# An encoder trunk's down-projection: the sums of its weights are transferred at half the rate

## The chip, the cores and the metric

The kernel runs on one core of a Trainium2 chip. The metric is the device time of one execution in microseconds. The time before is the median of three runs. A profile is one further execution, taken with the hardware profiler; its times count from the start of its span.

## The reference

Two layers of an encoder, on 512 tokens with 1024 channels, in float32. Each layer normalises x, makes one wide projection, runs four branches on it (a convolution and three kinds of attention), weighs each branch with gates from the same projection, adds them, projects once more and adds the result to x. A feed-forward part follows:

```python
def _conv_ffn(h, w_up, conv_w, conv_b, w_down):
    u = _depthwise_conv(h @ w_up, conv_w, conv_b)
    gate, up = jnp.split(u, 2, axis=-1)
    return (jax.nn.silu(gate) * up) @ w_down

# in each layer:
    branch = jnp.einsum('bsnc,ncd->bsnd', ys, w_branch[l])
    gates = jax.nn.sigmoid(gate_pre.reshape(bsz, seq, N_BRANCH, D_MODEL) + gate_b[l])
    mixed = jnp.sum(gates * branch, axis=2)
    x = x + mixed @ w_out[l]
    x = x + _conv_ffn(_rmsnorm(x, g_ffn[l]), w_up[l], ffn_conv_w[l], ffn_conv_b[l], w_down[l])
```

`w_down` is 2816 x 1024. The change concerns sums of blocks of this matrix, which the kernel makes because it multiplies blocks in a scheme with seven products instead of eight.

## The kernel before

**Products.** A float32 operand is split into a high part that TensorE takes exactly and a low part that holds the rest, and each product is three matmuls: high x high, high x low, low x high (`prod`, L273 to L275). A *block* is one unit of weights (128 x 1024) against all eight tiles of the activations: 24 matmuls of 512 columns. Weights come through the SP queue (L248) into two buffers, ScalarE makes the high part (L252), VectorE the low part (L254).

**The down-projection's sums.** `w_down` is held in eleven slabs of 128 rows by 2048 columns, each made of four blocks of 512 columns, b11, b12, b21 and b22. The scheme of seven products needs four sums of them in each slab: s3 = b12 + b11, s1 = b11 + b21, s2 = s3 + b21 and s4 = s2 + b22. They don't depend on the data, but they are made on the chip, from DRAM to DRAM: a plain transfer writes the first term, an accumulating transfer adds the next. `weight_sums` issues them for three chunks, of 4, 4 and 3 slabs, so that a transfer moves 512, 512 or 384 rows of 512 numbers: 1, 1 and 0.75 MB. A layer has 24 of them: in this order three for s3 = b12, three for s1 = b11, three that add b11 to s3, three that add b21 to s1, three copies s2 = s3, three that add b21, three copies s4 = s2, three that add b22. All go through GpSimd's queue (L1133), and since they belong to one queue, whatever GpSimd has to wait for before it issues one holds up all that stands behind it there. `quarter_sums` (L1110) does the like for the up-projection, 40 transfers a layer, and comes first.

**What sets the order.** The kernel is written as one main sequence of TensorE's work with generators at its side. After each half block the main sequence calls `tick`, and `tick` lets each generator in the list `side` take one step; what the step records stands at that place in the program. `slowly` wraps both generators of sums. It lets twelve ticks go by, and then as many ticks after each transfer as the generator yields (one, where it yields nothing):

```python
    def slowly(self, g):
        for _ in range(12):
            yield
        for n in g:
            for _ in range(n or SLOW):
                yield
```

`paced` makes each transfer wait, on the chip, for the matmul that was recorded last before it. In `layer` the sums are put into `side` at the start of the attention stage. Then come the remaining projections, and three stages of gates, `gates(n)` for three of the four branches. After them stands `while self.side: self.tick()`: it calls `tick` again and again, with no work of TensorE between, until every generator in the list has ended. The fourth `gates` follows, then the output projection and the feed-forward part.

**What stands behind the sums on GpSimd.** `gates` makes, for each of eight tiles d, a block for the gate, and VectorE scales it (L849, `t`). Two blocks later `branch` multiplies the branch's output by its weights, VectorE joins gate and product (L878, again a `t`; there are two buffers of that kind), and the result is added to the running sum `mx` (L879). In the second and third stage, and in the fourth for d below 6, GpSimd does this addition. In the fourth stage ScalarE and VectorE then split the sum into `mh` and `ml` (L883, L884) for the output projection. TensorE's results stand in four PSUM banks of the kind `mm` until VectorE has read them.

Of the kernel before, what the change touches and what calls it, by code (L numbers as in the profile page):

```python
# [218 lines left out]
class Trunk:  # L219
# [911 lines left out]
    def weight_sums(self, l):  # L1131

        add = lambda *a, **k: self.paced(self.nc.gpsimd.dma_start(*a, **k))  # L1133
        items = []
        for c in range(0, NP2, CHUNK):
            n = min(CHUNK, NP2 - c)
            t = self.dram.tile([n * P, 4 * S], F32, name=f"sums{c}", tag=f"sums{c}", bufs=2)
            self.sums[l].append(t)
            src = self.all_quads[l][c * P:(c + n) * P]
            part = lambda x, i: x[:, i * S:(i + 1) * S]  # L1140
            items.append((part, t, src))
        s2, s1, s3, s4 = range(4)
        b11, b12, b21, b22 = range(4)
        for d, s in ((s3, b12), (s1, b11)):
            for part, t, src in items:
                add(part(t, d), part(src, s))
                yield 2
        for d, s in ((s3, b11), (s1, b21)):
            for part, t, src in items:
                add(part(t, d), part(src, s), accum_op=ALU.add)  # L1150
                yield 2
        for d, b, s in ((s2, s3, b21), (s4, s2, b22)):
            for part, t, src in items:
                add(part(t, d), part(t, b))
                yield 2
            for part, t, src in items:
                add(part(t, d), part(src, s), accum_op=ALU.add)
                yield 2

    def pair_tags(self, j):  # L1160

# [366 lines left out]
```

## Time and profile before

| | us |
|---|---|
| median of 3 runs | 1598.54 (1597.10 to 1599.13) |
| the profiled execution | 1600.03 |
| its span | 1598.3 |
| TensorE busy | 1547.3 (97%) |
| VectorE busy | 1252.9 (78%) |
| ScalarE busy | 895.3 (56%) |
| GpSimd busy | 204.3 (13%) |
| software queue of the DMA engines (GpSimd's) | 92.81 MB, 26.0% of 16 engines |
| hardware queue (SP's) | 212.10 MB, 41.6% |

In the profile PE is TensorE's matmul, PEld its weight load, DVE is VectorE, ACT ScalarE, POOL GpSimd and SP SyncE. A row of a timeline gives start and duration in us, the engine, the line and the tile that is written, and in brackets how long the engine sat idle before and what released it. The duration of a DMA row on POOL is the time to issue it, not to transfer it. A row of the DMA view gives the size of a transfer and the time from issue to landing. q0 is the queue of the transfers that GpSimd issues, q1 that of SyncE's.

### The profile page before, as it was taken

To read this page: it belongs to the slowest core of one execution; us is meant where nothing else is said; L and a number is where in the kernel's file an instruction comes from. 1 tells how busy PE (TensorE), PEld (TensorE's weight loads), DVE (VectorE), ACT (ScalarE), POOL (GpSimd) and SP (SyncE) were. 2 spreads that over 40 slices of the span, in tenths; PEclk is the share of its full clock that TensorE was granted. 3 is DMA by queue.
4 is the path that set the end of the run, shared out by engine and by line. 5 is a ranking of instruction groups with operands and counts; after the bars stand their busy time and mean duration, and the time that the engine had idled before them with its cause. 6 is when DMAs were issued, how large, how long until landed. Compare 5 with 4: busy or idle time off the path is not lost.

```text
span 1598.3 us, 21942 instructions
## 1 busy us (share of the span) xinstructions
PE 1547.3 (97%) x7842; PEld 1312.7 (82%) x7842; DVE 1252.9 (78%) x2114; ACT 895.3 (56%) x1504; POOL 204.3 (13%) x308
## 2 busy tenths in 40 slices
PE   9999999996999999999999999999969999899999
PEld 8888888884889988888888878888858898888887
DVE  6699988752689989895676989887446888899964
ACT  6778777332456655563557677763234555554642
POOL 0044112332100000000002231132221000000000
PEclk9999999998999999999999999999989999999999
DMA  7789786999654543366567978769986466633565
GB/s 234 225 226 244 190 204 191 214 230 231 202 177 132 175 160 128 93 202 203 178 195 224 242 208 198 197 186 234 245 204 222 158 166 187 185 122 104 174 215 172
DMA packets 124797, 306.84 MB, mean 192 GB/s; under 512 B 28176, under 2 KB 30096, under 8 KB 124688
## 3 DMA queue, kind: packets, MB, share of 16 engines
q1 hardware_dynamic: 93712, 212.10, 41.6%
q0 software_dynamic: 30688, 92.81, 26.0%
q8 instruction: 62, 1.02, 0.3%
q10 hardware_dynamic: 288, 0.52, 0.1%
q14 instruction: 47, 0.39, 0.1%
HBM read 287.56 MB, written 100.67 MB: 243 GB/s over the span
## 4 chain that ended last, share of the span: by engine, by line
PE 73%; DMA 10%; DVE 9%; ACT 5%; issue 2%; POOL 1%; ACTq 0%; DVEq 0%; POOLq 0%
PE mm L273 14%; PE mm L275 14%; PE mm L274 14%; PE aux L992 4%; DVE w_lo L254 3%; DMA w_raw<-W 3%; DMA w_raw<-qS 3%; DMA sums<-W 3%; PE aux L1224 2%; PE aux L1223 2%; PE aux L1225 2%; ACT w_hi L252 2%; PE mm L1224 2%; PE mm L1223 2%; PE mm L1225 2%
## 5 line engine op out<-in xcount | busy, mean ns | idle before, releaser
L252 ACT ACTIVATE w_hi<-w_raw 128x1024 fp32r<-128x1024 f32 (+1 forms) x335 | 350.6, 1047 | 360.9 <-PE mm L274 127.9
L254 DVE TENSOR_TENSOR w_lo<-w_raw,w_hi 128x1024 fp32r<-128x1024 f32 (+1 forms) x335 | 406.3, 1215 | 110.3 <-ACT w_hi L252 108.6
L273 PE MATMUL mm<-xh,w_hi 128*128 128x512 f32 x960 | 377.0, 393 | 28.1 <-DVE t L849 27.1
L275 PE MATMUL mm<-xh,w_lo 128*128 128x512 f32 x960 | 375.8, 391 | 0.0
L274 PE MATMUL mm<-xl,w_hi 128*128 128x512 f32 x960 | 375.4, 391 | 0.0
L273 PEld LDWEIGHTS mm<-xh,w_hi 128*128 128x128 f32 x960 | 181.2, 189 | 65.9 <-ACT w_hi L252 27.9
L275 PEld LDWEIGHTS mm<-xh,w_lo 128*128 128x128 f32 x960 | 180.8, 188 | 39.5 <-DVE w_lo L254 1.4
L274 PEld LDWEIGHTS mm<-xl,w_hi 128*128 128x128 f32 x960 | 181.3, 189 | 36.2
L992 PE MATMUL aux<-form,w_hi 128*128 128x256 f32 x640 | 117.2, 284 | 1.3 <-ACT w_hi L252 1.1
L992 PEld LDWEIGHTS aux<-form,w_hi 128*128 128x128 f32 x640 | 99.8, 192 | 2.3 <-ACT w_hi L252 2.1
L440 DVE SCALAR_TENSOR_TENSOR cv<-cv,prm 128x512 f32<-128x512 f32 x120 | 94.0, 783 | 0.7
L992 PE MATMUL aux<-form,w_lo 128*128 128x256 f32 x320 | 91.0, 285 | 2.5 <-DVE w_lo L254 2.5
L1033 ACT ACTIVATE cy<-U,prm 128x512 f32<-128x512 f32 x88 | 69.9, 806 | 26.2 <-DVE U L1017 14.3
L879 POOL TENSOR_TENSOR mx<-mx,t 128x512 f32<-128x512 f32 x44 | 63.1, 1440 | 133.6 <-DVE t L878 133.5
L502 PE MATMUL mm<-w_hi,xh 128*128 128x512 f32 x192 | 76.4, 398 | 0.4 <-DVE V L630 0.4
L503 PE MATMUL mm<-w_lo,xh 128*128 128x512 f32 x192 | 75.0, 390 | 0.0
L504 PE MATMUL mm<-w_hi,xl 128*128 128x512 f32 x192 | 74.8, 390 | 0.0
L1110 POOL DMA_DIRECT2D qS<-W x60 | 43.7, 728 | 218.0 <-PE aux L780 107.2
L767 ACT ACTIVATE e<-e,rl 128x256 f32<-128x256 f32 (+2 forms) x96 | 57.4, 598 | 22.0 <-DVE rl L766 21.5
L1034 DVE SCALAR_TENSOR_TENSOR cy<-U,prm,cy 128x512 f32<-128x512 f32 x88 | 64.7, 745 | 6.2 <-ACT cy L1033 6.2
L849 DVE TENSOR_TENSOR t<-mm,RB 128x512 f32<-128x512 f32 x64 | 43.8, 685 | 29.3 <-PE mm L275 29.2
L1035 DVE SCALAR_TENSOR_TENSOR cy<-U,prm,cy 128x512 f32<-128x512 f32 x88 | 64.8, 745 | 0.8
(339 smaller groups left out, 3193.0 us busy)
## 6 DMA issues: line engine op xcount, KB each, us to landing
w_raw<-W SPq DMA_DIRECT2D x213, 512.0 KB, 3.7
qS<-W POOLq DMA_DIRECT2D x60, 512.0 KB, 6.4
sums<-W POOLq DMA_DIRECT2D x24, 1024.0 KB, 13.7
w_raw<-qS SPq DMA_DIRECT2D x40, 512.0 KB, 3.5
w_raw<-W SPq DMA_DIRECT2D x66, 256.0 KB, 3.9
w_raw<-sums SPq DMA_DIRECT2D x44, 256.0 KB, 4.0
w_raw<-sums SPq DMA_DIRECT2D x22, 512.0 KB, 4.6
qS<-qS POOLq DMA_DIRECT2D x20, 512.0 KB, 4.8
```

The lines of the kernel that those rows point to most:

```text
L252: w = nc.scalar.activation(hi[:, s], raw[:, s], AF.Copy)
L254: nc.vector.tensor_tensor(lo[:, s], raw[:, s], hi[:, s].bitcast(F32), ALU.subtract)
L273: mm(ps, lhsT=wh, rhs=xh, start=start, stop=False)
L274: mm(ps, lhsT=wh, rhs=xl, start=False, stop=False)
L275: self.last_mm = mm(ps, lhsT=wl, rhs=xh, start=False, stop=stop)
L440: self.after_mm(v.scalar_tensor_tensor(acc, u[:, t:t + S], w(t), acc, ALU.mult, ALU.add))
L502: mm(pss[b], lhsT=self.Xh[k][:, t], rhs=hi[:, s], start=k == 0, stop=False)
L503: mm(pss[b], lhsT=self.Xh[k][:, t], rhs=lo[:, s], start=False, stop=False)
L504: self.last_mm = mm(pss[b], lhsT=self.Xl[k][:, t], rhs=hi[:, s], start=False, stop=k == KT - 1)
L992: self.last_mm = nc.tensor.matmul(o, lhsT=w[:, s], rhs=x, start=start and not (e or j or i), stop=j == 3 and i == 2, skip_group_check=True)
L1033: nc.scalar.activation(y, u[:, 1:513], AF.Identity, scale=w(1), bias=self.par('ffn_conv_b', c))
L1035: v.scalar_tensor_tensor(y, u[:, 2:514], w(2), y, ALU.mult, ALU.add)
```

## The change

In `weight_sums` each `yield 2` becomes `yield 4`: after each of the 24 transfers the generator lets four ticks go by instead of two.

```diff
         for d, s in ((s3, b12), (s1, b11)):
             for part, t, src in items:
                 add(part(t, d), part(src, s))
-                yield 2
+                yield 4
         for d, s in ((s3, b11), (s1, b21)):
             for part, t, src in items:
                 add(part(t, d), part(src, s), accum_op=ALU.add)
-                yield 2
+                yield 4
         for d, b, s in ((s2, s3, b21), (s4, s2, b22)):
             for part, t, src in items:
                 add(part(t, d), part(t, b))
-                yield 2
+                yield 4
             for part, t, src in items:
                 add(part(t, d), part(src, s), accum_op=ALU.add)
-                yield 2
+                yield 4
```

How this moves the instructions is seen on GpSimd's queue alone; on the other engines the same instructions stand in the same order. First the end of the three gate stages in layer 0, before the change. The three tiles sums_2681 to sums_2683 are the three chunks; `W` as source is a block of the weights, `sums` as source is a copy; PE_49 is the wait for a matmul, DMASW with a number the wait for an earlier transfer of this queue, DVE_49 the wait for VectorE:

```order
L1133 DMA sums_2681<-sums_2681 512x512 [waits DMASW0_49,PE_49]
L879 TENSOR_TENSOR mx<-mx,t_3629 128x512 [waits DVE_49]
L879 TENSOR_TENSOR mx<-mx,t_3707 128x512 [waits DVE_49]
L1133 DMA sums_2682<-sums_2682 512x512 [waits DMASW1_49,PE_49]
L879 TENSOR_TENSOR mx<-mx,t_3753 128x512 [waits DVE_49]
L879 TENSOR_TENSOR mx<-mx,t_3763 128x512 [waits DVE_49,Pool_49]
L1133 DMA sums_2683<-sums_2683 384x512 [waits DMASW2_49,PE_49]
L879 TENSOR_TENSOR mx<-mx,t_3773 128x512 [waits DVE_49]
L1133 DMA sums_2681<-W 512x512 [waits DMASW6_49]
L1133 DMA sums_2682<-W 512x512 [waits DMASW7_49]
L1133 DMA sums_2683<-W 384x512 [waits DMASW3_49,DMASW0_49]
```

The same place with the change:

```order
L1133 DMA sums_2681<-W 512x512 [waits DMASW2_49,DMASW0_49,PE_49]
L879 TENSOR_TENSOR mx<-mx,t_3623 128x512 [waits DVE_49]
L879 TENSOR_TENSOR mx<-mx,t_3701 128x512 [waits DVE_49]
L879 TENSOR_TENSOR mx<-mx,t_3746 128x512 [waits DVE_49]
L879 TENSOR_TENSOR mx<-mx,t_3756 128x512 [waits DVE_49,Pool_49]
L1133 DMA sums_2682<-W 512x512 [waits DMASW3_49,DMASW1_49,PE_49]
L879 TENSOR_TENSOR mx<-mx,t_3766 128x512 [waits DVE_49]
L1133 DMA sums_2683<-W 384x512 [waits DMASW4_49]
L1133 DMA sums_2681<-W 512x512 [waits DMASW5_49]
L1133 DMA sums_2682<-W 512x512 [waits DMASW6_49]
L1133 DMA sums_2683<-W 384x512 [waits DMASW7_49]
```

Where three copies of s2 stood among the additions, the 13th to the 15th transfer, now the 7th and the 8th stand. The rows without PE_49 are those that the loop behind the third stage records: before, they begin with the 16th transfer, now with the 9th.

The second place is where both end, in layer 0, on GpSimd's queue with the change; the first row is the copy that makes s4 for the first chunk, the 19th transfer:

```order
L1133 DMA sums_2681<-sums_2681 512x512 [waits DMASW4_49,DMASW1_49]
L1133 DMA sums_2682<-sums_2682 512x512 [waits DMASW5_49,DMASW2_49]
L1133 DMA sums_2683<-sums_2683 384x512 [waits DMASW3_49]
L1133 DMA sums_2681<-W 512x512 [waits DMASW4_49]
L1133 DMA sums_2682<-W 512x512 [waits DMASW5_49]
L1133 DMA sums_2683<-W 384x512 [waits DMASW6_49]
L879 TENSOR_TENSOR mx<-mx,t_3908 128x512 [waits DVE_49,Pool_49]
L879 TENSOR_TENSOR mx<-mx,t_3957 128x512 [waits DVE_49,Pool_49]
```

These rows are the same before and after: the 19th to the 24th transfer stand in one piece ahead of the first addition of the fourth gate stage, and each waits for a transfer that was issued three places ahead of it. In layer 1 the same rows stand in the same way.

## The prediction

> **What bounds the kernel now.** I read the page's busy times first, then what TensorE (PE) waited for, then a table of stretches, and then GpSimd (POOL) instruction by instruction at the one place where TensorE stands still. First the page, then the three largest rows of TensorE's waits over the whole span (total us, how often, longest):
>
> ```profile
> PE 1547.3 (97%) x7842; PEld 1312.7 (82%) x7842; DVE 1252.9 (78%) x2114; ACT 895.3 (56%) x1504; POOL 204.3 (13%) x308
> ```
>
> ```profile
> PE mm L273 <- DVE t L849: 27.1, 2, 14.9
> PE aux L992 <- DVE w_lo L254: 4.7, 8, 1.3
> PE mm L992 <- ACT w_hi L252: 3.3, 2, 1.8
> ```
>
> TensorE is the bound, and more than half of what it loses is two stalls of 14.9 and 12.2 us. The table of stretches (length, busy us of PE, PEld, DVE, ACT, POOL, granted clock, DMA share, GB/s) places them:
>
> ```profile
> 220.00:230.00 10.00, 10.00 (x52) 8.35 (x51) 8.56 (x20) 8.80 (x27) 2.32 (x3) 1.00 1.01 223
> ...
> 330.00:340.00 10.00, 10.00 (x45) 8.27 (x45) 7.61 (x10) 5.25 (x8) 4.21 (x4) 1.00 0.74 222
> ...
> 370.00:380.00 10.00, 0.00 (x0) 0.00 (x0) 0.00 (x0) 0.00 (x0) 3.99 (x5) 0.62 1.03 236
> ...
> 1160.00:1170.00 10.00, 1.21 (x6) 0.67 (x4) 0.00 (x0) 0.00 (x0) 3.65 (x5) 0.71 0.99 254
> ```
>
> From 220 to 340, where the sums of layer 0 are issued now, all twelve stretches of 10 us have TensorE busy throughout; a lighter load on the DMA engines has nothing to give there. At 370 TensorE, VectorE and ScalarE all stand still and only POOL and the DMA engines work; layer 1 repeats it at 1160. The timeline of POOL over the drain of layer 0 (start, duration, instruction, and in brackets its idle time and what ended it):
>
> ```profile
> 340.16 0.59 POOL L1133 DMA_DIRECT2D sums<-sums  x1
> 340.77 1.68 POOL L879 TENSOR_TENSOR mx<-mx,t 128x512 f32<-128x512 f32 x1
> 342.39 2.12 POOL L1133 DMA_DIRECT2D sums<-W  x2
> 347.02 0.95 POOL L1133 DMA_DIRECT2D sums<-W  x1 [2.51 <-DMA sums<-sums]
> 358.24 0.66 POOL L1133 DMA_DIRECT2D sums<-sums  x1 [10.26 <-DMA sums<-W]
> 365.40 0.65 POOL L1133 DMA_DIRECT2D sums<-sums  x1 [6.51 <-DMA sums<-W]
> 369.72 0.59 POOL L1133 DMA_DIRECT2D sums<-sums  x1 [3.67 <-DMA sums<-W]
> ...
> 378.41 0.95 POOL L1133 DMA_DIRECT2D sums<-W  x1 [1.09 <-DMA sums<-sums]
> 379.02 1.63 POOL L879 TENSOR_TENSOR mx<-mx,t 128x512 f32<-128x512 f32 x1
> ```
>
> Number a layer's 24 sum transfers 1 to 24, in the order of the code: 1-6 plain, 7-12 accumulating, 13-15 copies, 16-18 accumulating, 19-21 copies, 22-24 accumulating; each three are 1, 1 and 0.75 MB. The row at 340.16 is number 15, and 16 to 24 follow with nothing between them: the loop that ends the third gate stage empties the pacing generator at once. Each of them waits on POOL until an earlier transfer has landed, and behind number 24 stands the addition L879 of the last gate stage. From there the timelines of VectorE and TensorE carry it on:
>
> ```profile
> 357.50 0.68 DVE L878 SCALAR_TENSOR_TENSOR t<-th,mm 128x512 f32<-128x512 f32 x1
> 381.34 0.69 DVE L884 SCALAR_TENSOR_TENSOR ml<-mx,mh 128x512 fp32r<-128x512 f32 x1 [23.16 <-ACT mh L883]
> ```
>
> ```profile
> 367.44 0.39 PE L275 MATMUL mm<-yh,w_lo 128*128 128x512 f32 x1
> 382.78 0.77 PE L273 MATMUL mm<-xh,w_hi 128*128 128x512 f32 x1 [14.95 <-DVE t L849]
> ```
>
> VectorE gives its product at 358.2, then stands at L884, which needs ScalarE's L883, which needs POOL's L879. Everything later in VectorE's queue (the evacuations L849, the weight splits L254) stands behind it. TensorE goes on until its four PSUM banks are full, at 367.8, and comes back 3.8 us after POOL reaches L879. So **each us by which POOL comes later to that first L879 is a us of TensorE**, with no slack left.
>
> **The change part by part.** *What it moves.* A step after four half blocks stands where every second step stood: the rows of the order show number 8 in the place of number 15, the one at 340.16, in both layers. So 1 to 8 are paced and 9 to 24 are emptied at once: sixteen transfers, not nine. No transfer is added or taken away; on TensorE, VectorE, ScalarE and the SP queue every instruction stays in its place. The first reads of `sums` stay safe: the SP queue issues them here, 75 us behind L879, and both shift together, while 24 is issued just ahead of L879 and needs some 18 us:
>
> ```profile
> 454.35 0.86 SPq L248 DMA_DIRECT2D w_raw<-sums  x2
> ```
>
> ```profile
> sums<-W POOLq DMA_DIRECT2D x1, 768.0 KB, 17.6
> ```
>
> *What stands between 340.16 and L879.* Number 24 is issued when 21 has landed (it waits for the lane of 21; 378.0 and 378.41 above). Now the queue has to carry 15 to 21 in that time; then it has to carry 8 to 21. Added: 8 to 12, accumulating, 1 + 0.75 + 1 + 1 + 0.75 = 4.5 MB, and the copies 13 and 14, 2 MB.
>
> *What a MB costs.* For each transfer of the drain of layer 0, its row of the DMA view (size, us from issue to landing; number 17 from the chain of waits: start, us), in order 15, 16, 17, 18, 19, 20, 21:
>
> ```profile
> sums<-sums POOLq DMA_DIRECT2D x1, 768.0 KB, 6.5
> ...
> sums<-W POOLq DMA_DIRECT2D x1, 1024.0 KB, 15.4
> ...
> 343.05 21.96 DMA sums<-W
> ...
> sums<-W POOLq DMA_DIRECT2D x1, 768.0 KB, 22.3
> ...
> sums<-sums POOLq DMA_DIRECT2D x1, 1024.0 KB, 14.4
> ...
> sums<-sums POOLq DMA_DIRECT2D x1, 1024.0 KB, 10.5
> ...
> sums<-sums POOLq DMA_DIRECT2D x1, 768.0 KB, 8.3
> ```
>
> With the issue times above they land at 346.7, 357.8, 365.0, 369.3, 372.6, 375.9 and 378.0: one after the other, a queue that is never empty. So the cost of one is the distance between landings. Accumulating: 15 to 17 took 18.3 us for 2 MB, 9.2 us a MB; 16 to 17 alone 7.2; 17 to 18 took 4.3 us for 0.75 MB, 5.7 a MB. Copies: 369.3 to 378.0, 8.7 us for 2.75 MB, 3.2 a MB. Why the first are dear shows in the queues' share of the DMA engines (packets, MB, share), first from 346 to 358, then from 365 to 369:
>
> ```profile
> q0 software_dynamic: 654, 1.31, 77.0%
> q1 hardware_dynamic: 325, 1.17, 26.1%
> ```
>
> ```profile
> q0 software_dynamic: 394, 1.14, 110.7%
> q1 hardware_dynamic: 2, 0.00, 0.3%
> ```
>
> The weight loads (q1) compete until VectorE's stop has filled their buffers; then the sums have the engines alone. That many weight loads are made now and after the change, so the 6.5 MB that come on top fall into the time in which the queue is alone. I take the row of that time, 5.7 us a MB: 4.5 x 5.7 + 2 x 3.2 = 25.7 + 6.4 = **32 us in layer 0**. In layer 1 the same rows of timeline, chain and DMA view (18 issued at 1140.69, 21 at 1161.27):
>
> ```profile
> 1136.17 20.72 DMA sums<-W
> ```
>
> ```profile
> 1140.69 0.94 POOL L1133 DMA_DIRECT2D sums<-W  x1 [3.06 <-DMA sums<-sums]
> ...
> 1161.27 0.59 POOL L1133 DMA_DIRECT2D sums<-sums  x1 [3.32 <-DMA sums<-W]
> ```
>
> ```profile
> sums<-W POOLq DMA_DIRECT2D x1, 768.0 KB, 20.2
> ...
> sums<-sums POOLq DMA_DIRECT2D x1, 768.0 KB, 7.4
> ```
>
> 17 lands at 1156.9, 18 at 1160.9, 21 at 1168.7: 5.3 us a MB accumulating, 2.8 a copy; 4.5 x 5.3 + 2 x 2.8 = 23.9 + 5.6 = **29.5 us in layer 1**. Together 61 us.
>
> *Bounds.* From below, accumulating transfers that run at the copies' pace in the longer queue: 6.5 x 3.2 and 6.5 x 2.8, 39 us. From above, all 4.5 MB at the disturbed price of 9.2: 2 x (41.4 + 6.4), 96 us. I choose near the row of the undisturbed queue, since nothing runs beside it there.
>
> *What I cost at nothing.* The restart. The granted clock is already down to 0.62 in the present stall, and this stretch behind it pays for it today:
>
> ```profile
> 380.00:390.00 10.00, 7.22 (x25) 5.57 (x26) 6.04 (x8) 4.61 (x6) 2.28 (x3) 0.70 1.10 228
> ```
>
> A longer stall pays that once as well; were it not paid already, it would be some 0.3 x 7.2 = 2 us. The lighter DMA load from 220 to 340: TensorE has no idle time there to give back. Numbers 22 to 24 and the weight loads behind them meet as they do now, only later.
>
> The profiled execution took 1600.03 us; 1600.0 + 61 = 1661, and since it stands 1.5 above the median of the runs, **1660** for the median.
>
> **The rivals.** *A. The long queue goes faster.* For it: with five transfers in line instead of three, the read and write of an accumulation could overlap better; then 39 us, 1638. Against: the queue already had all of the engines' time, 110.7%, when it made 5.7 us a MB. The Trainium skill, "DMA: Bandwidth & Descriptors", section "Anatomy of one DMA — SWDGE (gpsimd) path", fits such a transfer by 2.0 us and its bytes over 436 GB/s, with no word on accumulation: an estimate from it is 6.8 million bytes / 436 GB/s = 16 us a layer, 1630 in all. By that figure, 0.75 MB behind another transfer would take 1.8 us; the trace has 4.3 for an accumulation, so it does not agree.
>
> *B. The disturbed price holds throughout.* If weight loads, or the source reads of deeper accumulations, keep the price at 7.2 to 9.2, the sum is 2 x (32.4 + 6.4) = 78 to 96 us, 1676 to 1694. Against: no weight can be loaded while VectorE stands.
>
> *C. The stalls go away (the other side).* Were numbers 9 to 24 to find their predecessors landed, they would cost POOL only their issue: sixteen at 0.6 to 1.0 us, some 14 us, from 342.9 to 357. That is when VectorE's product is ready, so L879 would not be late, both stalls would vanish, and the time would be 1598.5 - 27 = 1571. It decides as soon as 21 lands before 357. For it: 1 to 7 have had more time each to land. Against: 16, 19 and 22 each need the one before in the same chunk, and 19 to 21 cannot start before 16 to 18 have been carried, which alone took until 369.3 with less ahead of them.
>
> *D. The change does not reach the drain.* If the remaining steps were paced on through the last gate stage, POOL would have no block at all. The order excludes it: sixteen rows of sums ahead of L879.
>
> **How the numbers follow.** The forecast, 1648 to 1674: 0.72. A, around 1638: 0.10. B, 1676 to 1694: 0.15. C and D, not slower: 0.03. The range 1643 to 1682 leaves out most of A, the dearer half of B, and C, not quite 2 in 10. A measurement of this kernel tells a difference of about 0.2%, 3 us, from no change; every case but C and D is far beyond it: slower 0.97, within 0.2% 0.01, faster 0.02.
>
> **What would show it.** TensorE's wait for L849 should again be two, near 47 and 42 us, some 88 in all instead of 27.1, and no other wait should have grown. POOL should issue an accumulating transfer where it now issues the copy at 340.16, then its first L879 of the last gate stage near 379 + 32 = 411. In layer 1 number 21 should land near 1168.7 + 61.5 = 1230. Number 21 should land about 70 us behind number 8's issue, not 38. The landings of 9 to 18 with the hardware queue silent show the price: 5.3 to 5.7 us a MB is the forecast, near 3 is A, over 7 is B. I am wrong in kind if TensorE idles elsewhere, or if POOL reaches L879 before 379.

## The result, and the profile after

With one transfer per four half blocks the kernel takes 1663.2 us (median of four runs, 1660.2 to 1664.9) against 1598.8 for the kernel before on the same chip: 1.0402 times as long, with an interval of 1.0383 to 1.0421. The profiled execution took 1664.91 us, its span 1663.1.

The page of the changed kernel and TensorE's largest waits:

```profile
PE 1549.0 (93%) x7842; PEld 1313.8 (79%) x7842; DVE 1252.5 (75%) x2114; ACT 895.2 (54%) x1504; POOL 204.9 (12%) x308
```

```profile
PE mm L273 <- DVE t L849: 88.5, 2, 44.4
PE aux L992 <- DVE w_lo L254: 5.3, 7, 1.3
PE aux L992 <- ACT w_hi L252: 4.3, 6, 1.0
```

TensorE's work is what it was, 1549 us. The wait for L849 has gone from 27.1 to 88.5 us, and it is still two stalls: 44.4 us in layer 0, and so 44.1 in layer 1. These 61.4 us are 95% of the 64.8 by which the span has grown; of the other 3.4, 1.7 are busy time and the rest small waits.

The same stretch of GpSimd as before, from the last paced transfer (number 8) to the first addition of the fourth gate stage:

```profile
336.83 1.02 POOL L1133 DMA_DIRECT2D sums<-W  x1
337.51 1.66 POOL L879 TENSOR_TENSOR mx<-mx,t 128x512 f32<-128x512 f32 x1
339.06 3.10 POOL L1133 DMA_DIRECT2D sums<-W  x3
352.11 0.95 POOL L1133 DMA_DIRECT2D sums<-W  x1 [9.94 <-issue]
356.02 1.32 POOL L1133 DMA_DIRECT2D sums<-sums  x2 [2.97 <-issue]
364.44 0.59 POOL L1133 DMA_DIRECT2D sums<-sums  x1 [7.10 <-issue]
376.94 1.05 POOL L1133 DMA_DIRECT2D sums<-W  x1 [11.90 <-DMA sums<-sums]
...
381.27 0.95 POOL L1133 DMA_DIRECT2D sums<-W  x1 [0.82 <-DMA sums<-sums]
389.51 0.66 POOL L1133 DMA_DIRECT2D sums<-sums  x1 [7.29 <-DMA sums<-W]
...
398.43 0.59 POOL L1133 DMA_DIRECT2D sums<-sums  x1 [3.17 <-DMA sums<-W]
...
406.96 0.95 POOL L1133 DMA_DIRECT2D sums<-W  x1 [1.09 <-DMA sums<-sums]
407.57 1.62 POOL L879 TENSOR_TENSOR mx<-mx,t 128x512 f32<-128x512 f32 x1
```

Number 8 is issued at 336.8, 9 to 24 follow with only the third stage's last addition ahead of them, and the first L879 of the fourth stage starts at 407.6 instead of 379.0. VectorE and TensorE of the changed kernel show the same chain as before, only longer:

```profile
354.12 0.68 DVE L878 SCALAR_TENSOR_TENSOR t<-th,mm 128x512 f32<-128x512 f32 x1
409.89 0.69 DVE L884 SCALAR_TENSOR_TENSOR ml<-mx,mh 128x512 fp32r<-128x512 f32 x1 [55.09 <-ACT mh L883]
```

```profile
366.50 0.39 PE L275 MATMUL mm<-yh,w_lo 128*128 128x512 f32 x1
411.33 0.76 PE L273 MATMUL mm<-xh,w_hi 128*128 128x512 f32 x1 [44.44 <-DVE t L849]
```

TensorE comes to its stop at 366.9, at the same place of the program as before and a us earlier in time; it was that us ahead already when the first sum was issued (226.8 against 227.8). It starts again 3.8 us behind L879, as it did.

The landings, from the DMA view of the changed kernel (size, us from issue to landing): numbers 8, 12, 13, 15, 16, 18 and 21 of layer 0.

```profile
sums<-W POOLq DMA_DIRECT2D x1, 1024.0 KB, 15.0
...
sums<-W POOLq DMA_DIRECT2D x1, 768.0 KB, 21.8
...
sums<-sums POOLq DMA_DIRECT2D x1, 1024.0 KB, 20.5
...
sums<-sums POOLq DMA_DIRECT2D x1, 768.0 KB, 16.4
...
sums<-W POOLq DMA_DIRECT2D x1, 1024.0 KB, 12.2
...
sums<-W POOLq DMA_DIRECT2D x1, 768.0 KB, 16.8
...
sums<-sums POOLq DMA_DIRECT2D x1, 768.0 KB, 8.1
```

With the issue times they land at 351.8 (8), 373.9 (12), 380.8 (15), 398.1 (18) and 406.5 (21). From 8 to 12, 3.5 MB accumulating take 22.1 us, 6.3 a MB; the copies 13 to 15 take 6.9, 2.5 a MB; 16 to 18, with nothing else on the engines, 17.3, again 6.3 a MB (8.3 of them for number 16, which follows copies, and then 5.1 a MB for 17 and 18); 19 to 21 take 8.4, 3.1 a MB. From the issue of 8 to the landing of 21 it is 69.7 us.

### The profile page after: what moved, and what is told of

It reads as the page before. It is cut to its first block, busy times and chain, and to the rows that moved or that the text cites. A ratio compares the mean times of both kernels' runs of the same rounds, so it can differ in the third digit from the quotient of the medians.

```text
span 1663.1 us, 21928 instructions
## 1 busy us (share of the span) xinstructions
PE 1549.0 (93%) x7842; PEld 1313.8 (79%) x7842; DVE 1252.5 (75%) x2114; ACT 895.2 (54%) x1504; POOL 204.9 (12%) x308
## 3 DMA queue, kind: packets, MB, share of 16 engines
q0 software_dynamic: 30688, 92.81, 25.2%
## 4 chain that ended last, share of the span: by engine, by line
PE 71%; DMA 12%; DVE 7%; ACT 5%; issue 3%; POOL 2%; ACTq 0%; DVEq 0%; POOLq 0%
PE mm L273 14%; PE mm L275 14%; PE mm L274 14%; DMA sums<-sums 4%; DMA w_raw<-qS 4%; DVE w_lo L254 3%; PE aux L992 3%; PE aux L1225 2%; PE aux L1223 2%; PE aux L1224 2%; DMA w_raw<-W 2%; ACT w_hi L252 2%; PE mm L1225 2%; PE mm L1223 2%; PE mm L1224 2%
## 5 line engine op out<-in xcount | busy, mean ns | idle before, releaser
L273 PE MATMUL mm<-xh,w_hi 128*128 128x512 f32 x960 | 377.5, 393 | 89.7 <-DVE t L849 88.5
L884 DVE SCALAR_TENSOR_TENSOR ml<-mx,mh 128x512 fp32r<-128x512 f32 x16 | 11.0, 690 | 124.6 <-ACT mh L883 124.3
L879 POOL TENSOR_TENSOR mx<-mx,t 128x512 f32<-128x512 f32 x44 | 65.1, 1486 | 156.8 <-DVE t L878 141.9
L883 ACT ACTIVATE mh<-mx 128x512 fp32r<-128x512 f32 x16 | 10.0, 627 | 135.9 <-POOL mx L879 131.4
L1034 DVE SCALAR_TENSOR_TENSOR cy<-U,prm,cy 128x512 f32<-128x512 f32 x88 | 64.6, 745 | 6.2 <-ACT cy L1033 6.2
L767 ACT ACTIVATE e<-e,rl 128x256 f32<-128x256 f32 (+2 forms) x96 | 57.3, 597 | 22.1 <-DVE rl L766 21.6
```

The lines of the kernel that those rows point to most:

```text
L273: mm(ps, lhsT=wh, rhs=xh, start=start, stop=False)
```

## The experiments

The question for the first group is whether TensorE stands because of GpSimd's queue, or because sixteen transfers load the DMA engines.

**The fourth stage's additions on VectorE**, in the changed kernel and in the kernel before:

```diff
-        (v if n == ORDER[3] and d >= 6 else nc.gpsimd).tensor_tensor(m, m, t, ALU.add)
+        (v if n == ORDER[3] else nc.gpsimd).tensor_tensor(m, m, t, ALU.add)
```

> The changed kernel, but the additions L879 of the fourth gate stage are all made by VectorE instead of six of eight by GpSimd. The sixteen transfers that are emptied at once stay. Theory (TensorE stands because L879 is queued on GpSimd behind transfers that wait for each other): TensorE's wait for L849, 88.5 us, goes to under 4 us, and the time is 1663.2 - 88.5 + some 2 for VectorE's additions, 1570 to 1582. Rival (the sixteen transfers starve the weight loads, and TensorE would stand with or without GpSimd): the wait moves to w_hi or w_lo and the time stays above 1630.

> The same move of the additions in the kernel before, with one transfer per two half blocks. Theory: its two stalls, 27.1 us, go as well: 1598.8 - 27.1 + some 2, 1570 to 1578, and the difference to the run with one per four half blocks is under 5 us instead of 64. Rival (weight loads starved): at most 10 us are won.

Measured: 1595.9 us with one per four half blocks, 1.0001 times the kernel before (0.9988 to 1.0013); 1573.8 with one per two, 0.9858 (0.9840 to 0.9875). In both the wait for L849 is gone from TensorE's list, whose longest row is now, for one per four:

```profile
PE mm L273 <- ACT xh L335: 8.2, 4, 3.0
PE aux L992 <- DVE w_lo L254: 5.1, 7, 1.3
```

So the stall did hang on GpSimd's queue, and for the kernel before the theory has the size too. In the changed kernel it has not: 1570 to 1582 was expected, and the two differ by 22 us instead of under 5. The transfers are still emptied at once, and now the output projection runs beside them. The weight loads between 385 and 440, first with one per four, then with one per two (count, size, median us to landing):

```profile
w_raw<-W SPq DMA_DIRECT2D x9, 512.0 KB, 10.0
```

```profile
w_raw<-W SPq DMA_DIRECT2D x10, 512.0 KB, 4.5
```

The weight loads take twice as long. Slower still are the loads of x to which the output projection's result is added, and on which the products of the row above hang: 12.2 us against 3.5. The two profiled executions are 16.1 us apart; 10.9 of these are waits of TensorE and 5.2 busy time (1552.8 us against 1547.6), in part at a lower clock: from 440 to 455 the clock granted to TensorE is 0.74 with one per four and 1.00 with one per two. The rival, load on the DMA engines, is thus no cause of the 88.5 us. It is, as far as these longer loads show, what the next 20 hang on, hidden as long as TensorE stood; no run takes that load away alone.

**Spreading the transfers past the end of the third stage**, by twos and by fours: the generator of the sums, `slow`, is held while the loop empties the list, and goes on in the fourth stage.

```diff
+                held = slow in self.side
+                if held:
+                    self.side.remove(slow)
                 while self.side:
                     self.tick()
+                if held:
+                    self.side.append(slow)
```

> The kernel before, but the generator of sums is taken out of the list while the loop behind the third gate stage empties it, and put back for the fourth: numbers 15 to 24 go on, one per two half blocks, between the additions of the fourth stage. Theory: no addition stands behind more than two or three transfers, most of which find their predecessors landed; both stalls fall under 4 us; 1570 to 1580. Rival (the transfers beside the fourth stage's weight loads cost TensorE as much, wherever GpSimd stands): 1590 or more.

> The changed kernel with the same hold: one per four half blocks, and really so to the end, so that numbers 13 to 24 come beside the up-projection. Theory: the rate as such costs nothing, only the emptying does: 1570 to 1582, with TensorE's wait for L849 under 4 us. Rival (one per four half blocks makes the sums late for the down-projection's first loads): a new wait for the loads of sums, and 1590 or more.

Measured: 1594.1 us by twos (0.9980 of the kernel before, 0.9970 to 0.9989), and 1648.9 by fours (1.0322, 1.0298 to 1.0346). Both expectations missed the time, though the wait for L849 is gone from both. By twos, TensorE's list is headed by a new row, and GpSimd's timeline shows where it comes from:

```profile
PE mm L273 <- DVE U L1070: 20.5, 2, 10.7
```

```profile
390.24 1.30 POOL L879 TENSOR_TENSOR mx<-mx,t 128x512 f32<-128x512 f32 x1 [4.18 <-DVE t L878]
438.05 1.05 POOL L1133 DMA_DIRECT2D sums<-W  x1 [46.52 <-DVE xl L336]
438.71 0.50 POOL L1058 MEMSET U<- 128x2 f32 x1
...
438.85 4.25 POOL L943 DMA_DIRECT2D xf<-res  x7
...
453.29 1.01 POOL L1133 DMA_DIRECT2D sums<-W  x1 [0.25 <-issue]
```

Number 22 was the last to find a tick in the fourth stage; the one at 438, of 1024 KB, is number 23, and the one at 453, of 768 KB, is 24. There are no ticks in the output projection, so 23 is paced by a matmul of the up-projection's beginning, and GpSimd stands 46.5 us for it. Behind it wait the loads `xf`, which VectorE needs ahead of the up-projection's first results. It is the same mechanism in a second place, and this time it was the edit that made it.

By fours, thirteen transfers are left for the up-projection. On the first, number 12, GpSimd stands the same 46.5 us, and the sums come late. The queue of SyncE waits for one of them, 11.8 us in layer 0 and 10.1 in layer 1, and its weight loads stand behind that wait; TensorE's list begins with a product of the up-projection:

```profile
SPq L248 <- DMA sums<-W: 11.8, 1, 11.8
```

```profile
PE aux L992 <- ACT sv L1004: 28.1, 5, 11.0
PE mm L273 <- DVE U L1070: 17.2, 2, 9.1
```

So the rival named for this run came true: one per four half blocks does end too late, if it is kept to the end. That the rate as such costs nothing was not shown: TensorE's busy time, too, is 21.5 us above that of the kernel before, at a mean granted clock of 0.976 instead of 0.991.

**The spread, closed**: as by twos, but what is left is issued right behind the fourth stage; and the same with the additions on VectorE.

```diff
                 self.gates(ORDER[3])
+                while slow in self.side:
+                    self.tick()
```

> The kernel before with its transfers spread through the fourth gate stage, as in the run that spread them by twos, but the one that was left over there (number 24, which stood on GpSimd for 46.5 us waiting for its matmul, ahead of the memsets and the loads that the up-projection needs) is issued right behind the fourth stage. Theory (that left-over block is the same mechanism at a second place, and is all that the spread lost): TensorE's wait for L1070, 20.5 us, goes under 3 us, and the time is 1594.1 - 20.5 = 1573.6, within 4 us. Rival (the spread loses the rest by load on the DMA engines): 1585 or more.

> The same, and the fourth stage's additions all on VectorE. Theory (each of the two cures removes the same 27.1 us of stalls, so they don't add): 1570 to 1576, no more than 3 us from either alone. Rival (spreading also relieves the weight loads of the fourth stage): 1568 or less.

The transfer that stood for 46.5 us was number 23, as its size shows; two were left over, 23 and 24, and here both are issued at 391.3, right behind the stage's last addition on GpSimd.

Measured: 1568.0 us (0.9831, 0.9816 to 0.9846) and 1568.8 (0.9837, 0.9819 to 0.9854). Both are below their windows, by 1.6 and 1.2 us. What neither sum counted is TensorE's busy time, 1544.1 and 1543.1 us, which in the run by twos was 1549.4: without stalls it has been spared the slow clock behind them (mean granted clock 0.999, by twos 0.991). The waits of the first:

```profile
PE aux L992 <- DVE w_lo L254: 4.8, 6, 1.3
PE aux L992 <- ACT w_hi L252: 4.4, 6, 1.1
```

In the list of GpSimd's waits ahead of L1133 there is no landing any more, only TensorE's pace and this row:

```profile
  issue: 2.8, 10
```

The two cures don't add, as expected: the times are 0.8 us apart, within the scatter of the runs. They are the fastest kernels of the study; the first, 27.3 us below the kernel before that ran beside it (1595.3), only moves one generator past one loop and empties it behind the next stage.

The second group measures how the stall depends on what is left to carry.

**One per three, and one per one half block**: the number in `yield` alone.

> One transfer per three half blocks: ten are paced, and 11 to 24 are emptied at once. Theory (the stall is what the queue still has to carry): against the kernel before, numbers 10, 11 and 12 (2.75 MB accumulating, 6.3 us a MB as measured in the changed kernel) and 13 and 14 (2 MB copies, 2.8 us a MB) are added behind the last paced one, less the 2.7 us by which number 10 is issued earlier: 17.3 + 5.6 - 2.7 = 20 us a layer, 1640, with TensorE's wait for L849 at 67 us. Rival (a fixed price for any slower pace): 1663 as with four.

> One transfer per half block: all 24 are paced and nothing is left for the loop that empties the generator. Theory: GpSimd reaches the fourth stage's first addition at once and the wait for L849 goes under 6 us: 1572 to 1590, the upper half if additions of the third stage get stuck behind transfers that come faster than the queue carries them. Rival (dense transfers crowd out the weight loads of the second and third stage): new waits for w_hi, 1600 or more.

Measured for three: 1634.0 us, with

```profile
PE mm L273 <- DVE t L849: 61.1, 2, 32.3
```

that is between two (27.1) and four (88.5), 6 us below what was expected: a stall that grows with the MB left over, not a fixed price. For one: 1600.1 us, 1.0019 (1.0002 to 1.0035) of the kernel before. The wait for L849 is 3.1 us, as the theory has it, but the time lies above its window and just where the rival had it. The rival's sign is missing all the same: TensorE's waits for `w_hi` are 7.4 us, against 6.5 in the kernel before. The transfers now come faster than the queue carries them (at 303.9 one has stood 14.0 us for a landing), and additions of the third stage stand behind them; VectorE waits for GpSimd to free its buffers `t`, and TensorE for VectorE:

```profile
DVE t L878 <- POOL mx L879: 36.3, 8, 10.3
```

```profile
PE aux L478 <- DVE cv L469: 15.8, 2, 8.0
```

Again the same coupling, a stage earlier.

**No accumulation**: the 24 transfers of a layer are all plain, so this kernel leaves out the sums and only moves their bytes; the edit stands at two places.

```diff
-                add(part(t, d), part(src, s), accum_op=ALU.add)
+                add(part(t, d), part(src, s))
```

> The changed kernel with plain transfers in place of the twelve accumulating ones of each layer, so the sums are left out and only their bytes are moved; order, waits and sizes stay. Theory (the price is that of accumulating, 6 us a MB against 3 for copies): numbers 8 to 21, 12.75 MB, take some 40 us instead of 70, the wait for L849 falls from 88.5 to about 30, and the time to about 1603. Rival (the price lies in the number of transfers and GpSimd's waits, not in accumulating): 1650 or more.

Measured: 1623.4 us, and 49.6 us of waiting for L849: between the two. Numbers 8 to 21 took 50.4 us, where 40 was expected and 69.7 is the time with accumulation. The price of 16 to 18, the three that have the engines alone, is as the theory has it. In the DMA view, number 15 and then 18:

```profile
sums<-sums POOLq DMA_DIRECT2D x1, 768.0 KB, 19.5
...
sums<-W POOLq DMA_DIRECT2D x1, 768.0 KB, 7.9
```

Issued at 350.55 and 370.49, they land at 370.1 and 378.4: 8.3 us for 2.75 MB, 3.0 a MB, against 6.3 with accumulation. The Trainium skill, "Collectives: The Full Stack", section "The bandwidth ceiling: the fold count and why AG ≠ RS ≠ AR", says of ReduceScatter, a collective that adds in the DMA path, that it is the second read that halves the rate, not the adding. The ratio here, 2.1, agrees; why it is so, no run here shows. The traces show another difference that could give the same ratio: with and without accumulation GpSimd's queue moves the same 92.81 MB, but in 30688 packets against 25056, that is 5632 more, one for each 4 KB of the 22 MB that the two layers add. What I missed is the first part: 8 to 15 took 32.3 us from the issue of number 8 at 337.74. The weight loads have their share of it, 2.10 MB between 338 and 370, just as much as in the changed kernel.

**The memory for descriptors.** GpSimd's row at 352.11 waits 9.94 us for something named only issue. Halved, and doubled (for which one of two extra weight buffers of the down-projection had to go):

```diff
-    nc = _bacc.Bacc("TRN2", target_bir_lowering=False, num_devices=1, dynamic_dma_scratch_size=4096)
+    nc = _bacc.Bacc("TRN2", target_bir_lowering=False, num_devices=1, dynamic_dma_scratch_size=2048)
```

> The changed kernel with half the memory for the descriptors of GpSimd's transfers (2048 instead of 4096). In the changed kernel GpSimd waits 20.0 us in layer 0's emptying for something that the profile names only issue, ahead of numbers 12, 13 and 15. Theory (that is room for descriptors, and the DMA engines are busy meanwhile): these waits grow to 30 us or more, fewer transfers are in line, and the time stays within 8 us of 1663 because the queue is never empty. Rival (they are landings that the profile fails to name): the waits stay 20.0 us.

> The changed kernel with twice the memory for the descriptors of GpSimd's transfers (8192 instead of 4096); to make room, the extra weight buffers of the down-projection are one instead of two, which may cost a few us there. Theory (the wait named issue is room for descriptors): GpSimd's 39.2 us of waits named issue over both layers go under 5 us. With four accumulations in line the engines were already full (105%), so the time from the issue of number 8 to the landing of number 21, 69.7 us in layer 0, stays within 4 us, and TensorE's wait for L849 within 8 us of 88.5. Rival (more in line would go faster still, as half the memory went slower): the 69.7 us fall under 64 and the wait under 78.

The waits ahead of L1133 by that name, over both layers: changed kernel, then half the memory.

```profile
  issue: 39.2, 6
```

```profile
  issue: 130.3, 14
```

With twice the memory there is no such row. So it is room for descriptors. With twice the memory L849 stands for 87.1 us, and number 8 is issued at 337.36 and 21 lands at 406.9, 69.5 us: a longer line goes no faster, which answers the prediction's rival A. (That kernel takes 1708.2 us in all. It loses 22.0 us in waits for `w_hi` in the down-projection, and 16.7 us of busy time; as GpSimd issues nothing there, I put that down to the missing weight buffer, which no run takes away alone.) With half the memory the theory was wrong on the time: 1702.7 us, and 128.3 us of waiting for L849. Fewer in line do not keep the engines full. The software queue's packets, MB and share while 16 to 18 are carried, with half the memory (384 to 409) and in the changed kernel (381 to 398):

```profile
q0 software_dynamic: 1591, 3.76, 90.7%
```

```profile
q0 software_dynamic: 1543, 3.39, 105.4%
```

## Why the prediction was right

*The bound and the chain* held. The stalls sit where they sat, the bulk of TensorE's idle time is again two waits for L849 (88.5 of 114.1 us), and both vanish when L879 no longer stands in GpSimd's queue behind the transfers.

*What is moved*: number 8 stands in the place of 15, sixteen are emptied at once, and it is they that decide: the run with three gives a stall between those with two and four.

*The price.* The term of layer 0 came out: from the issue of 8 to the landing of 21 it is 69.7 us, 31.8 more than the 37.9 from 15 to 21 before, where the term said 32. It isn't made up as I had it, though. Numbers 8 to 12, from the issue of 8, took 37.1 us for their 4.5 MB, 8.2 a MB and not 5.7. In exchange 16 to 18 took 17.3 us, where before they took 22.6, from 346.7 to 369.3. The weight loads that press on the queue meet 8 to 12 now (the hardware queue has 27.9% of the DMA engines from 346 to 358) and met 16 to 18 before (26.1%). That no more of them come is what I had argued (2.10 MB between 338 and 374, against 2.20 between 340 and 366 before), and that is why the difference holds while the price of the single transfers does not. The term of layer 1 was too small. There the rows are, for numbers 8 and 21:

```profile
1161.13 1.01 POOL L1133 DMA_DIRECT2D sums<-W  x1
...
1221.61 0.59 POOL L1133 DMA_DIRECT2D sums<-sums  x1 [2.50 <-DMA sums<-W]
```

```profile
sums<-sums POOLq DMA_DIRECT2D x1, 768.0 KB, 8.9
```

Number 21 lands at 1230.5, 69.4 us behind the issue of 8, where 35.4 + 29.5 = 64.9 was forecast.

*What was luck.* TensorE's stalls grew by 29.5 us in layer 0, where the sum has 32, and by 31.9 in layer 1, where it has 29.5. In layer 0 I had number 8 issued at 340.16, in the place of 15; it was issued 3.3 us earlier, so L879 came at 407.6 and not at 411. In layer 1 the price was too low by 4.5 us, of which an earlier issue of number 8 gave back a part. Each layer by itself is thus off by some 2.5 us, and that they add up to 61.4 against a sum of 61 is chance. The forecast of 1660 is 3 us short of 1663 because busy time and small waits also grew, which I had put at nothing.

*What I cost at nothing.* That the stretch from 220 to 340 has nothing to give holds: the us by which TensorE is ahead at 366.9 it had at the first sum already. That a longer stall pays for the clock only once holds nearly: TensorE's busy time grew by 1.7 us. The load on the DMA engines was rightly left out, but only since the stall covers it: with the additions on VectorE, where nothing covers it, the slower pace costs some 20 us.

*The rivals.* A is answered by the large memory, and by 6.3 us a MB with the engines at 105%. B, the disturbed price throughout, did not come: beside the weight loads 8 to 12 cost 8.2, but 17 and 18, alone in the queue, 5.1. C asked for transfers that find their predecessors landed; it happens when they are spread, and the stalls then do vanish: 1568, where C had said 1571. D the order had excluded, and GpSimd's rows show the block.

## What to carry to other kernels

A transfer that an engine issues is also a place in that engine's queue. Count, for each loop that empties a generator at the end of a stage, what stands behind what it issues, and price it by what the transfers still have to carry, not by how long they take to issue; a slower pace makes that block longer, not shorter. If work that was paced is to be moved past such a loop, look for the next thing behind it in the same queue too: here it cost 20.5 us at the very next stage.

## What was unexpected of the hardware

GpSimd could not issue a fifth accumulating transfer while four, of 0.75 to 1 MB, were in line: number 12 is issued at 352.1, when 8 has landed at 351.8. The wait for it carries no engine's name in the profile: 39.2 us in the changed kernel, 130.3 with half the memory for descriptors, none with twice. With half of it the same transfers needed more time, too. There number 15 is the row at 380.97, and 21, which waits for 18, the one at 413.54; the DMA view has 15's landing:

```profile
380.97 0.59 POOL L1133 DMA_DIRECT2D sums<-sums  x1 [3.00 <-issue]
...
413.54 0.59 POOL L1133 DMA_DIRECT2D sums<-sums  x1 [3.22 <-DMA sums<-W]
```

```profile
sums<-sums POOLq DMA_DIRECT2D x1, 768.0 KB, 8.3
```

Number 15 lands at 389.3 and 18 just ahead of 413.5, some 24 us for 16 to 18 instead of 17.3. Of the three sizes that were run, the two larger carry 8 to 21 at the same rate (69.7 and 69.5 us) and only the smallest is slower: here the room for descriptors limits the rate once too few transfers are in line to keep the DMA engines full.
